# A hybrid encoder trunk on one core: a third unit of seven block products in each feed-forward layer, and the units spread over the second to sixth chunk

## The chip, the core and the metric

The kernel runs on one core of a Trainium2 chip. The metric is the device time of one execution in microseconds (us): 2188.74 is the median of three runs of the kernel before (2188.52 to 2188.94). The engines are TensorE (PE, matmuls; PEld is its loading of stationary operands), VectorE (DVE), ScalarE (ACT), GpSimd (POOL) and SyncE (SP, which issues the transfers of weights here). Each engine executes its own program in order, and engines wait for each other by semaphores.

## What is computed

Two layers on 256 tokens of width 2048: the first mixes by pooling and grouped-query attention, the second by a bidirectional mLSTM. Each is followed by a gated feed-forward part (FFN) with a depthwise convolution over three neighbouring tokens. All data is float32. The change touches the up-projection of the FFN alone:

```python
def conv_ffn(x, w_up, conv_w, conv_b, w_down):      # D_MODEL 2048, D_FF 5632
    u = x @ w_up                                    # (256, 2048) @ (2048, 2*5632)
    up = jnp.pad(u, ((0, 0), (1, 1), (0, 0)))
    u = c[0] * up[:, :-2] + c[1] * up[:, 1:-1] + c[2] * up[:, 2:] + conv_b
    gate, val = jnp.split(u, 2, axis=-1)
    return (jax.nn.silu(gate) * val) @ w_down       # (256, 5632) @ (5632, 2048)

for layer in range(2):
    ...
    x = x + mixed
    x = x + conv_ffn(rms_norm(x, norm_ffn[layer]), w_up[layer], ...)
```

## The kernel before

**Products in two parts.** Every float32 operand is split into a high part, which a matmul takes exactly, and the low rest. A product is three matmuls: high by high, high by low and low by high. For weights this is `Stream` (L65): it issues a chunk of 128 x 1024 weights (512 KB) on SP's queue into a tile `w` (L89), ACT copies the high part into `hl` (L112), and DVE subtracts to get the low part (L113). In the FFN seven chunks are loaded ahead and three split ahead of the one that PE uses (L1103); the chunks come in the order in which PE needs them.

**The FFN.** The 5632 inner columns are 44 *row tiles* of 128; a row tile is a gate part and a value part. They are cut into six K chunks of 4, 8, 8, 8, 8 and 8 row tiles (`FCH`, L33; numbered 0 to 5), since they are what the down-projection sums over. `up` (L928) computes one row tile for all 256 tokens with the weights stationary: 16 blocks of the width 2048, each with two matmuls of 512 columns and two of 256, 64 in all, four weight chunks. ACT and DVE then gather the sums (L391, L392), multiply by the tokens' norm (L936), and `tail` (L912) does the convolution, the gate and the split of the result (L917 to L926) into a gate tile `g`. `down` (L1074) multiplies a chunk's gate tiles with the down weights, in four blocks of 512 output columns, and adds into `x` (L401). Gate tiles of even and odd chunks use two buffers in turn (B0, B1).

**Units of seven products.** For four of a chunk's row tiles another way is there, `quads` (L978). It takes the tokens in two halves and the blocks of the width in pairs, so that the product is one of 2 x 2 blocks, and computes it with seven block products instead of eight, from sums of blocks. The sums of activations `sx` are made once for each layer by DVE and ACT (`sums`, L939, with L945 to L961), the sums of weights by DVE in the loaded chunk (`sums` of `Stream`, L93: a chunk of kind "sum" takes one addition of 512 columns, L99; one of kind "chain" two, L102 and L103). A unit has eight pairs of blocks in 28 *steps* of one weight chunk each: 16 of four products (p1, p5 and p6, p4 in turn, a chunk each), and 12 of the three others. A step is six matmuls of 512 columns. A unit's 28 chunks stand in place of the 16 of four row tiles. Its result comes out with the tokens on the partitions, in four accumulators that DVE and ACT combine (L1006 to L1027); `finish` (L1032) turns it by 16 transposes on PE, copies (L1041) and calls the same `tail`. A unit begins only when the tails of the one before are done (`late`, L991).

**The order.** PE's program is in the order in which the code is written (`manual_schedule`, L206). For the FFN `_ffn_plan` (L1192) writes it as a list: a *slot* is a quarter of a row tile (16 matmuls) or two blocks of a down-projection (12 matmuls), and after each slot stand the unit steps that fall to it. `UNITS` (L1189) has a unit for the last four row tiles of chunks 2 and 4, each with the chunk and the offset in slots where its steps begin and end; the steps are spread evenly between. The sequence of weight chunks follows the same plan (`_ffn_order`, L1239). Work of other engines that belongs to PE's progress is fed in by `Weave` (L135), a list of small tasks that come due while PE's program is written. The order of DVE's and ACT's instructions is set by the framework's scheduler from these programs; only the sums of weights and activations are pinned to the order of the code.

Of the kernel before, what the change touches and what calls it, by code (L numbers as in the profile page):

```python
# [10 lines left out]
F32R = mybir.dt.float32r  # L11
# [5 lines left out]
P = 128  # L17
D = 2048
S = 256
# [161 lines left out]
def trunk(ctx: ExitStack, tc: tile.TileContext, gx, xT, xn, call, catt, cml, weights, out):  # L181
    nc = tc.nc
    v, a, g, pe = nc.vector, nc.scalar, nc.gpsimd, nc.tensor
# [713 lines left out]
    def ffn_layer(layer, norm, nxt):  # L897
        with ExitStack() as es:
# [76 lines left out]
            def sum_of(j, p):  # L975
                return [sx[:, j, p, i, :] for i in range(2)]

            def quads(fs, gt, i0, name):  # L978

                def bank(j):  # L980
                    return psp.tile([P, 512], F32, tag="ps", name=f"p{j}_{name}")
# [29 lines left out]
                for p in range(m):  # L1011
                    hl = st.next()
                    product(b5, sum_of(3, p), hl, 0, False, p == m - 1)
                    product(b6, sum_of(2, p), hl, 512, False, p == m - 1)
                    if p == m - 1:
                        v.scalar_tensor_tensor(c21, b6, r1, c21, ALU.mult, ALU.add)
                        v.tensor_add(c22, c22, c21)
                        v.scalar_tensor_tensor(c21, b4, r1, c21, ALU.mult, ALU.subtract)
                        v.scalar_tensor_tensor(c12, b5, n0, c12, ALU.mult, ALU.add)
                    yield  # L1020
                    if p % 2:
                        hl = st.next()
                        for n in range(2):
                            product(b1, block_of(2 * (p - 1 + n) + 1, 0), hl, n * 512, False, p - 1 + n == m - 1)
                        if p == m - 1:
                            c11 = part(11)
                            a.activation(c11, b1, AF.Copy, scale=r0)  # L1027
                            wv.add(finish(c12, c22, fs[2:], gt, i0 + 2, name), 3.0)
                            wv.add(finish(c11, c21, fs[:2], gt, i0, name), 5.0)
                        yield  # L1030

            def finish(top, bottom, fs, gt, i0, name):  # L1032

                for n, f in enumerate(fs):
                    tr = psp.tile([P, 2, S], F32, tag="ps", name=f"tr{layer}_{f}")
                    for j in range(2):
                        for t, src in enumerate((top, bottom)):
                            c = (2 * j + n) * P
                            pe.transpose(tr[:, j, t * P : t * P + P], src[:, c : c + P], ident)
                    u = tp.tile([P, 2, S], F32, tag="tb", name=f"tb_{layer}_{f}")  # L1040
                    a.copy(u, tr)  # L1041
                    tail(u, f, gt, i0 + n)
                    yield 2.5
                late.discard((i0 - 4) % 4)
# [57 lines left out]
            wv.add(sums_ready(), 14.0)  # L1102
            st.la, st.sa, st.more = 7, 3, (lp(f"fw{layer}", 1), lp(f"fh{layer}", 1), st.at + len(_ffn_plan()))  # L1103
            gts, run, late = {}, {}, set()
            for step in _ffn_plan():
                kind, c = step[:2]
                if kind != "d" and c not in gts:
                    gts[c] = actp.tile([P, 8, 2, S], F32R, tag=f"B{c % 2}", name=f"g{layer}_{c}")
                key = step[:3]
                if key not in run:  # L1110
                    f0 = sum(FCH[:c])
                    run[key] = (up(f0 + step[2], gts[c], step[2]) if kind == "n" else
                                down(c, gts[c], step[2]) if kind == "d" else
                                quads([f0 + 4 + j for j in range(4)], gts[c], 4, f"{layer}_{c}"))
                next(run[key], None)
            for e in run.values():
                assert next(e, None) is None
# [68 lines left out]
    return np.concatenate(out)  # L1186


UNITS = {2: (1, 2, 3, -7), 4: (3, 2, 5, -7)}  # L1189


def _ffn_plan():  # L1192
# [168 lines left out]
```

## Time and profile before

| What | Value |
|---|---|
| Median of the runs | 2188.74 us |
| The profiled execution | 2188.64 us |
| Its span, from first to last instruction | 2186.3 us |
| Packets of SP's queue (the weights), share of 16 transfer engines' time | 61.4% |
| Traffic, mean over the span | 202 GB/s |
| Time to landing of a unit's 512 KB chunk, median | 4.0 us |
| Matmuls of the units (all kinds), now four units | 672 |
| First FFN layer's up-projection begins | at 255.94 us |

The profile is one execution on the chip. A busy time is the sum over an engine's instructions with overlaps counted once; matmul records overlap, since matmuls are pipelined, so lengths of PE's work are read from the chain of waits or from start to start. "idle before, releaser" is the time that an engine stood still just before a group, and what ended it. Names such as `hl` or `p` are tiles of the program with their numbers left out: `up` is the accumulator of a row tile, `dn` of a down-projection, `p` of a unit, `tr` of its transposes, `hl` a split weight chunk. L227 is the line of a helper that writes every matmul.

### The profile page before, as it was taken

The page shows a single profiled execution, that of the slowest core. Times are in us where ns is not written, and L with a number is a line of the kernel's source. Part 1 is how long each engine was busy: PE and PEld are TensorE (multiplying, and loading weights), DVE is VectorE, ACT ScalarE, POOL GpSimd, SP SyncE. Part 2 cuts the span into 40 slices and gives each one's busy share as a digit, 9 for nine tenths or more (in the row PEclk, how much of TensorE's full clock was granted, in tenths as well). Part 3 has the DMA queues.
Part 4 walks back from the last instruction along what each step waited for, and adds up shares of the span by engine and source line. Part 5 has one row for each costly group of instructions (what it writes and reads, how often), then busy time and mean ns, then how long its engine had stood idle before and what let it go on. Part 6 is the DMA issues. An engine that isn't in the chain of part 4 may idle for free.

```text
span 2186.3 us, 30347 instructions
## 1 busy us (share of the span) xinstructions
PE 2180.1 (100%) x11328; PEld 1861.1 (85%) x11328; DVE 1673.3 (77%) x2378; ACT 1229.4 (56%) x1744; POOL 29.2 (1%) x40
## 2 busy tenths in 40 slices
PE   9999999999999999999999999999999999999999
PEld 7888888888888888889888888888888888888887
DVE  7686798878887786666767676679987888778664
ACT  7665565656555565556555554556565655556552
POOL 0020000000000000000000000000000000000000
PEclk9999999999999999999999999999999999999999
DMA  9555557675676755557565555655677667676563
GB/s 323 181 168 174 183 186 231 229 230 195 229 226 221 226 195 192 186 161 205 160 202 179 181 179 176 196 183 181 233 231 226 198 220 233 221 222 196 193 189 125
DMA packets 124950, 440.88 MB, mean 202 GB/s; under 512 B 13850, under 2 KB 16194, under 8 KB 124802
## 3 DMA queue, kind: packets, MB, share of 16 engines
q1 hardware_dynamic: 121568, 434.93, 61.4%
q10 hardware_dynamic: 3074, 3.75, 0.8%
q8 instruction: 89, 1.46, 0.3%
q14 instruction: 59, 0.48, 0.1%
q0 software_dynamic: 160, 0.26, 0.0%
HBM read 436.74 MB, written 2.14 MB: 201 GB/s over the span
## 4 chain that ended last, share of the span: by engine, by line
PE 97%; DVE 2%; issue 0%; ACT 0%
PE up L227 34%; PE dn L227 21%; PE op L227 8%; PE p L227 7%; PE mv L227 4%; PE mq L227 4%; PE mk L227 4%; PE mo L227 4%; PE qproj L227 3%; PE pool L227 1%; PE kproj L227 1%; PE vproj L227 1%; DVE hl L113 1%; PE av L227 1%; PE qk L227 1%; PE end L227 0%
## 5 line engine op out<-in xcount | busy, mean ns | idle before, releaser
L113 DVE TENSOR_TENSOR hl<-w,hl 128x1024 fp32r<-128x1024 f32 (+1 forms) x820 | 992.6, 1218 | 357.6 <-ACT hl L112 350.8
L112 ACT CAST hl<-w 128x1024 fp32r<-128x1024 f32 (+1 forms) x819 | 852.4, 1048 | 662.1 <-PE up L227 137.3
L227 PE MATMUL up<-xx,hl 128*128 128x512 f32 (+1 forms) x4608 | 823.1, 337 | 0.0
L227 PEld LDWEIGHTS up<-xx,hl 128*128 128x128 f32 x4608 | 716.1, 188 | 109.1
L227 PE MATMUL dn<-hl,g 128*128 128x512 f32 x2064 | 480.9, 390 | 0.0
L227 PEld LDWEIGHTS dn<-hl,g 128*128 128x128 f32 x2064 | 385.0, 188 | 78.5
L227 PE MATMUL p<-hl,sx 128*128 128x512 f32 x384 | 103.5, 391 | 1.1 <-DVE hl L113 1.1
L391 ACT COPY tb_up<-up 128x512 f32<-128x512 f32 x72 | 42.2, 587 | 99.4 <-PE up L227 94.8
L917 ACT ACTIVATE y<-tb_up,cst 128x256 f32<-128x256 f32 x144 | 78.8, 595 | 32.6 <-DVE tb_up L936 30.4
L227 PE MATMUL mk<-xx,hl 128*128 128x512 f32 (+1 forms) x512 | 92.2, 338 | 0.0
L227 PE MATMUL mq<-xx,hl 128*128 128x512 f32 (+1 forms) x512 | 92.2, 337 | 0.0
L227 PE MATMUL mv<-hl,xx 128*128 128x512 f32 (+2 forms) x480 | 91.7, 350 | 0.0
L227 PE MATMUL op<-hl,cat 128*128 128x512 f32 x384 | 91.6, 393 | 0.0
L227 PE MATMUL mo<-hl,xx 128*128 128x512 f32 x384 | 90.5, 391 | 0.0
L227 PE MATMUL op<-hl,mcat 128*128 128x512 f32 x384 | 89.5, 392 | 0.0
L227 PEld LDWEIGHTS mq<-xx,hl 128*128 128x128 f32 x512 | 79.3, 188 | 11.6
L227 PEld LDWEIGHTS mk<-xx,hl 128*128 128x128 f32 x512 | 79.1, 188 | 11.4
L227 PEld LDWEIGHTS mv<-hl,xx 128*128 128x128 f32 x480 | 78.3, 189 | 11.2
L392 DVE TENSOR_TENSOR tb_up<-up,tb_up 128x512 f32<-128x512 f32 x72 | 49.8, 692 | 47.7 <-ACT tb_up L391 47.6
L227 PEld LDWEIGHTS op<-hl,mcat 128*128 128x128 f32 x384 | 71.5, 188 | 14.6
L227 PEld LDWEIGHTS mo<-hl,xx 128*128 128x128 f32 x384 | 71.0, 188 | 14.3
L227 PEld LDWEIGHTS op<-hl,cat 128*128 128x128 f32 x384 | 70.9, 188 | 14.1
(240 smaller groups left out, 1740.2 us busy)
## 6 DMA issues: line engine op xcount, KB each, us to landing
w<-in_up SPq DMA_DIRECT2D x288, 512.0 KB, 4.2
w<-in_dn SPq DMA_DIRECT2D x176, 512.0 KB, 4.2
w<-in_m_in SPq DMA_DIRECT2D x124, 512.0 KB, 4.1
w<-in_q SPq DMA_DIRECT2D x112, 512.0 KB, 4.0
w<-in_a_in SPq DMA_DIRECT2D x46, 512.0 KB, 4.4
w<-in_a_out SPq DMA_DIRECT2D x32, 512.0 KB, 3.4
w<-in_m_out SPq DMA_DIRECT2D x32, 512.0 KB, 3.4
w<-in_m_g SPq DMA_DIRECT2D x5, 432.0 KB, 3.5
```

The source lines that it names most:

```text
L112: (self.nc.vector.tensor_copy if i + c == 0 else self.nc.scalar.copy)(hl[:, 0, c : c + n], w[:, c : c + n])
L113: self.nc.vector.tensor_sub(hl[:, 1, c : c + n], w[:, c : c + n], hl[:, 0, c : c + n].bitcast(F32))
L227: pe.matmul(out_, lhsT, rhs, start=start, stop=stop, skip_group_check=True)
L391: a.copy(tb, ps[:, :, 1, :])
L392: v.tensor_add(tb, ps[:, :, 0, :], tb)
L917: a.activation(y[:, j, :], u[:, j, :], AF.Identity, scale=cw(tl, 1), bias=cw(tl, 3))
```

## The change

The change puts a third unit into each layer, for the last four row tiles of chunk 5, and gives all three new places: the first from two slots into chunk 1 to slot 20 of chunk 2, the second from slot 23 of chunk 2 to slot 2 of chunk 4, the third from slot 5 of chunk 4 to slot 24 of chunk 5. The last two slots in each entry of `UNITS` count from the start of the chunk named; before, -7 was seven slots ahead of it. A layer has then 84 steps and 216 slots where it had 56 and 232. The gate tile of a chunk is no longer taken at the first step that belongs to the chunk, but where it is first written (`g_of`).

```diff
-            def quads(fs, gt, i0, name):
+            def quads(fs, c, i0, name):
...
                             a.activation(c11, b1, AF.Copy, scale=r0)
+                            gt = g_of(c)
                             wv.add(finish(c12, c22, fs[2:], gt, i0 + 2, name), 3.0)
                             wv.add(finish(c11, c21, fs[:2], gt, i0, name), 5.0)
...
             gts, run, late = {}, {}, set()
+            def g_of(c):
+                if c not in gts:
+                    gts[c] = actp.tile([P, 8, 2, S], F32R, tag=f"B{c % 2}", name=f"g{layer}_{c}")
+                return gts[c]
+
             for step in _ffn_plan():
                 kind, c = step[:2]
-                if kind != "d" and c not in gts:
-                    gts[c] = actp.tile([P, 8, 2, S], F32R, tag=f"B{c % 2}", name=f"g{layer}_{c}")
                 key = step[:3]
                 if key not in run:
                     f0 = sum(FCH[:c])
-                    run[key] = (up(f0 + step[2], gts[c], step[2]) if kind == "n" else
+                    run[key] = (up(f0 + step[2], g_of(c), step[2]) if kind == "n" else
                                 down(c, gts[c], step[2]) if kind == "d" else
-                                quads([f0 + 4 + j for j in range(4)], gts[c], 4, f"{layer}_{c}"))
+                                quads([f0 + 4 + j for j in range(4)], c, 4, f"{layer}_{c}"))
                 next(run[key], None)
...
-UNITS = {2: (1, 2, 3, -7), 4: (3, 2, 5, -7)}
+UNITS = {2: (1, 2, 2, 20), 4: (2, 23, 4, 2), 5: (4, 5, 5, 24)}
```

What this does to the order is seen at three places. The first two are DVE's program where the first unit of the first layer begins, from the low half of chunk hl100 on. Names carry the chunk's number: hl101 is the split of w101, and so on; v0 and sx0 are the sums of activations. Before:

```order
L113 TENSOR_TENSOR hl100_2904<-w100_2795,hl100_2904 128x1024
L961 TENSOR_TENSOR sx0_2407<-v0_2595,sx0_2407 128x4x128 x2
L926 TENSOR_TENSOR g0_0_2415<-y0_2_2760,g0_0_2415 128x256
L956 TENSOR_TENSOR v0_2595<-v0_2595 128x512
L961 TENSOR_TENSOR sx0_2407<-v0_2595,sx0_2407 128x4x128
L936 TENSOR_TENSOR tb_up0_3_2862<-tb_up0_3_2862,R1_2530 128x512
L113 TENSOR_TENSOR hl101_2928<-w101_2818,hl101_2928 128x1024
L102 TENSOR_TENSOR w102_2840<-w102_2840,w99_2772 128x512
L961 TENSOR_TENSOR sx0_2407<-v0_2595,sx0_2407 128x4x128
L918 SCALAR_TENSOR_TENSOR y0_3_2866<-tb_up0_3_2862,cst_84,y0_3_2866 128x255 x2
L103 TENSOR_TENSOR w102_2840<-w102_2840 128x512
L113 TENSOR_TENSOR hl104_3006<-w104_2902,hl104_3006 128x1024
```

Here the unit's second chunk is w102, two quarter tiles after the first, w99. The same place after the change:

```order
L113 TENSOR_TENSOR hl100_2904<-w100_2795,hl100_2904 128x1024
L102 TENSOR_TENSOR w101_2818<-w101_2818,w99_2772 128x512
L961 TENSOR_TENSOR sx0_2407<-v0_2595,sx0_2407 128x4x128 x2
L926 TENSOR_TENSOR g0_0_2415<-y0_2_2760,g0_0_2415 128x256
L956 TENSOR_TENSOR v0_2595<-v0_2595 128x512
L961 TENSOR_TENSOR sx0_2407<-v0_2595,sx0_2407 128x4x128
L936 TENSOR_TENSOR tb_up0_3_2862<-tb_up0_3_2862,R1_2530 128x512
L103 TENSOR_TENSOR w101_2818<-w101_2818 128x512
L961 TENSOR_TENSOR sx0_2407<-v0_2595,sx0_2407 128x4x128
L918 SCALAR_TENSOR_TENSOR y0_3_2866<-tb_up0_3_2862,cst_84,y0_3_2866 128x255 x2
L920 SCALAR_TENSOR_TENSOR y0_3_2866<-tb_up0_3_2862,cst_84,y0_3_2866 128x255 x2
L113 TENSOR_TENSOR hl101_2930<-w101_2818,hl101_2930 128x1024
```

The second chunk is now w101, after one quarter tile; its two sums stand ahead of the last of sx, and its low half behind two L918 and two L920. In the second layer the rows are the same up to L103; then the low half of the chunk after the unit's second one (hl564) comes first, behind it the last sx and two L918, then that of the unit's second chunk (hl563), and the L920 behind that. DVE's program of the first layer goes on, after the change, with:

```order
L113 TENSOR_TENSOR hl102_2951<-w102_2840,hl102_2951 128x1024
L113 TENSOR_TENSOR hl103_2966<-w103_2879,hl103_2966 128x1024
L99 TENSOR_TENSOR w104_2902<-w104_2902 128x512
L392 TENSOR_TENSOR tb_up0_4_2988<-up0_4_2878,tb_up0_4_2988 128x512
L113 TENSOR_TENSOR hl105_3019<-w105_2928,hl105_3019 128x1024
L924 TENSOR_TENSOR y0_3_2866<-y0_3_2866 128x256
L113 TENSOR_TENSOR hl106_3042<-w106_2949,hl106_3042 128x1024
L102 TENSOR_TENSOR w107_2964<-w107_2964,w104_2902 128x512
L936 TENSOR_TENSOR tb_up0_4_2988<-tb_up0_4_2988,R1_2530 128x512
L113 TENSOR_TENSOR hl104_3005<-w104_2902,hl104_3005 128x1024
```

The unit's third chunk is w104, and its low half stands behind those of hl105 and hl106, which PE uses later. Before, the third was w105, and the row was hl102, hl103, hl105.

The third place is PE's program in chunk 5 of the first layer, at the second block of chunk 4's down-projection (`dn_4_1`). Before, the four blocks of it stood together:

```order
L227 MATMUL up_39_7523<-xx_126,hl_7526 128x256 x2
L227 MATMUL dn_4_1_7623<-hl_7547,g_4_5020 128x512 x12
L227 MATMUL dn_4_1_7623<-hl_7568,g_4_5020 128x512 x12
L227 MATMUL dn_4_1_7623<-hl_7589,g_4_5020 128x512 x12
L227 MATMUL dn_4_1_7623<-hl_7626,g_4_5020 128x512 x12
L227 MATMUL up_40_7694<-xx_126,hl_7643 128x512 x2
```

After the change steps of the third unit stand between them, and fewer row tiles around them:

```order
L227 MATMUL up_37_7570<-xx_126,hl_7606 128x256 x2
L227 MATMUL dn_4_1_7694<-hl_7627,g_4_6381 128x512 x12
L227 MATMUL p_0_5_6610<-hl_7648,xx_126 128x512 x6
L227 MATMUL dn_4_1_7694<-hl_7659,g_4_6381 128x512 x12
L227 MATMUL p_0_5_6611<-hl_7697,sx_2407 128x512 x3
L227 MATMUL p_0_5_6641<-hl_7697,sx_2407 128x512 x3
L227 MATMUL dn_4_1_7694<-hl_7714,g_4_6381 128x512 x12
L227 MATMUL dn_4_1_7694<-hl_7725,g_4_6381 128x512 x12
```

Each of the steps is a chunk more for SP, ACT and DVE in front of the next slot.

## The prediction

> **What bounds the kernel now.** I read the clock first, then the page's busy shares and its chain of waits, then the groups, then the timelines of TensorE (PE) and VectorE (DVE) around the units of seven products.
>
> ```profile
> core 0: 2186.3 us, clock 1.000
> PE 2180.1 (100%) x11328; PEld 1861.1 (85%) x11328; DVE 1673.3 (77%) x2378; ACT 1229.4 (56%) x1744; POOL 29.2 (1%) x40
> PE 97%; DVE 2%; issue 0%; ACT 0%
> L227 PE MATMUL p<-hl,sx 128*128 128x512 f32 x384 | 103.5, 391 | 1.1 <-DVE hl L113 1.1
> L113 DVE TENSOR_TENSOR hl<-w,hl 128x1024 fp32r<-128x1024 f32 (+1 forms) x820 | 992.6, 1218 | 357.6 <-ACT hl L112 350.8
> ```
>
> The granted clock is full, PE is busy all of the span, and 97% of the chain that ended last is PE. Both feed-forward (FFN) layers are a stream of matmuls with hardly a hole, so the time is PE's work plus what PE waits for. Among the units' products PE idles 1.1 us in all, and what ends the idling is DVE, making the low half of a weight chunk (L113). DVE is the runner-up: its 77% is an average, and in the first unit's stretch it is more:
>
> ```profile
> 310.20:515.10 204.90, 204.37 (x1055) 174.05 (x1053) 175.07 (x231) 119.20 (x151) 0.00 (x0) 1.00 0.71 227
> ```
>
> The columns are the stretch, its length, then busy time of PE, its weight loads, DVE, ACT and POOL, then clock, DMA share and GB/s. DVE is busy 175.1 of 204.9 us there (85%), ACT 58%. So every edit has two prices: PE time, which is the span, and DVE time, which becomes the span where DVE falls behind by more than the chunks split in advance.
>
> **What a unit saves on PE.** The chain of waits lists pieces (start, length, what) so that lengths add up without the overlap of matmul records:
>
> ```profile
> 340.21 5.56 PE up L227 x32
> 345.77 1.37 PE p L227 x6
> 347.14 5.56 PE up L227 x32
> 352.70 1.37 PE p L227 x6
> ```
>
> Half a row tile of the plain up-projection (32 matmuls) takes 5.56 us, so a tile 11.12 and the four tiles that a unit replaces 44.48. One step of a unit (a chunk, six matmuls) takes 1.365 (these two pieces read 1.37, others 1.36); 28 steps take 38.22. A unit also needs 16 transposes, which the plain tiles do not. PE's timeline where the first unit's are threaded into a tile:
>
> ```profile
> 517.82 0.85 PE L227 MATMUL up<-xx,hl 128*128 128x512 f32 x4
> 518.50 0.60 PE L1039 MATMUL tr<-cst,c 128*128 128x128 f32 x4
> 518.86 2.35 PE L227 MATMUL up<-xx,hl 128*128 128x512 f32 x12
> ...
> 524.75 0.60 PE L1039 MATMUL tr<-cst,c 128*128 128x128 f32 x4
> 525.11 5.13 PE L227 MATMUL up<-xx,hl 128*128 128x512 f32 x28
> ```
>
> Four groups of four transposes stand behind 4, 12, 4 and 12 up matmuls (the rows left out are the middle ones). From 517.82 to 525.11 are 7.29 us; the 32 up matmuls are half a tile, 5.56, so the 16 transposes cost 1.73. One unit in place of four tiles therefore saves 44.48 - 38.22 - 1.73 = 4.53 us of PE, and one per layer in two layers 9.06. This is the first term and the certain one: the products are the same instructions, and the last chunk's down-projections are untouched.
>
> The Trainium skill (TensorE: Matmul & The Clock Gate, Back-to-back issue gap) gives 512/2.4 + 2.5 = 216 ns and 109 ns for 256 columns. The trace's steps are longer (1.365 us over six is 0.2275). By the page a tile would be an estimated 10.40 us, a step 1.30, the saving 41.6 - 36.3 - 1.73 = 3.6 per unit, and the sum below 1.9 us less gained; rows decide.
>
> **What else a unit adds.** Twelve more chunks per unit pass SP's queue, ACT's cast, and DVE's subtraction, and 32 sums of 512 columns run on DVE. Removed with four tiles are four gathers (L391, L392) and four multiplications (L936). Whether that is hidden is DVE's question. The densest new stretch is the third unit: 28 steps over 51 quarter-tile slots, where the first unit now has 28 over 63. DVE's prices, from start to start, are in this timeline (start, length, then the instruction):
>
> ```profile
> 305.46 1.22 DVE L113 TENSOR_TENSOR hl<-w,hl 128x1024 fp32r<-128x1024 f32 x1
> 306.60 1.29 DVE L961 TENSOR_TENSOR sx<-v,sx 128x512 fp32r<-128x512 f32 x2
> 307.80 0.42 DVE L926 TENSOR_TENSOR g<-y,g 128x256 fp32r<-128x256 f32 x1
> 308.14 0.69 DVE L956 TENSOR_TENSOR v<-v 128x512 f32<-128x512 f32 x1
> ...
> 309.94 1.22 DVE L113 TENSOR_TENSOR hl<-w,hl 128x1024 fp32r<-128x1024 f32 x1
> 311.08 0.69 DVE L102 TENSOR_TENSOR w<-w,w 128x512 f32<-128x512 f32 x1
> 311.68 0.69 DVE L961 TENSOR_TENSOR sx<-v,sx 128x512 fp32r<-128x512 f32 x1
> 312.28 0.88 DVE L918 SCALAR_TENSOR_TENSOR y<-tb_up,cst,y 128x255 f32<-128x255 f32 x2
> ...
> 316.80 3.49 DVE L113 TENSOR_TENSOR hl<-w,hl 128x1024 fp32r<-128x1024 f32 x3
> ```
>
> So a subtraction takes 1.14 (309.94 to 311.08), an addition of 512 columns 0.60, two L918 0.79, an L926 or L924 0.34. The unit's own work is 28 x 1.14 + 32 x 0.60 = 51.1 us. The other 175.1 - 51.1 = 124.0 us of the first unit's stretch belong to 63 slots; 51 slots carry 100.4, so DVE has 151.5 us to do in the third unit's stretch. PE's time for it: (204.9 - 38.2) x 51/63 + 38.2 = 173.1. DVE would be at 88% there, ACT at 59% by the same scaling. The 79 chunks of 0.524 MB ask 239 GB/s, against 227 in the row above, and the page's slices show more than that without a wait for a transfer:
>
> ```profile
> GB/s 323 181 168 174 183 186 231 229 230 195 229 226 221 226 195 192 186 161 205 160 202 179 181 179 176 196 183 181 233 231 226 198 220 233 221 222 196 193 189 125
> ```
>
> So on average the added work lies beside PE: I cost it at nothing, but for two kinds of place, where DVE's work comes in a lump.
>
> **The starts of the first unit.** Here DVE also makes the sums of the activations (sx), and here PE waits today, once in each layer, at the unit's second step:
>
> ```profile
> 310.22 0.85 PE L227 MATMUL p<-hl,xx 128*128 128x512 f32 x3
> 310.91 0.84 PE L227 MATMUL p<-hl,sx 128*128 128x512 f32 x3
> 311.59 5.72 PE L227 MATMUL up<-xx,hl 128*128 128x512 f32 x32
> 317.15 0.40 PE L227 MATMUL p<-hl,sx 128*128 128x512 f32 x1
> 318.08 0.74 PE L227 MATMUL p<-hl,sx 128*128 128x512 f32 x2 [0.53 <-DVE hl L113]
> ```
>
> Matmuls of a product start 0.23 apart (0.69 for three); here 0.93 lie between the first and the second, so 0.70 are lost: the second matmul needs the low half, which DVE's L113 of 316.80 delivers at 318.02. The change brings the second step one quarter tile (2.78) nearer, and the order of DVE changes with it. I lay the new order (shown with the change) on today's prices, from the last instruction that both share (hl100, 305.46). Ahead of hl101 now stand L102 0.60, two sx 1.20, L926 0.34, L956, sx, L936, L103 and sx 0.60 each, 0.79 for two L918 and as much for two L920: it starts at 306.60 + 6.72 = 313.32 and ends at 314.54. PE's second step is due at 311.59 + 2.78 = 314.37, its second matmul at 314.60: no wait. PE leaves it at 315.74 and needs hl104 after two quarter tiles, at 321.30, the low half at 321.53. DVE starts hl104 last of a row: hl101, hl102, hl103, hl105, hl106 at 1.14, four of 0.60 (L99, L392, L102, L936) and L924, thus 313.32 + 5.70 + 2.40 + 0.34 = 321.76, and ends at 322.98. PE waits 1.45 there in place of 0.70.
>
> ```profile
> 1509.07 1.22 DVE L113 TENSOR_TENSOR hl<-w,hl 128x1024 fp32r<-128x1024 f32 x1
> ...
> 1513.82 0.85 PE L227 MATMUL p<-hl,xx 128*128 128x512 f32 x3
> ...
> 1520.75 0.40 PE L227 MATMUL p<-hl,sx 128*128 128x512 f32 x1
> 1521.68 0.72 PE L227 MATMUL p<-hl,sx 128*128 128x512 f32 x2 [0.53 <-DVE hl L113]
> ```
>
> The second layer (rows of DVE and PE together) loses 0.70 today too. There the second step's hl563 now stands behind hl564: hl562 is done with DVE's front at 1509.07 + 1.14 = 1510.21, hl563 starts 5.93 + 1.14 = 7.07 later and ends at 1518.50; the second matmul is due at 1513.82 + 1.37 + 2.78 + 0.23 = 1518.20, a wait of 0.3. What comes after I bound by nothing and by the first layer's 1.45, and take 0.7: a wait of about 1.0 in all. Together 2.45 where 1.40 are lost now: **+1.05**. The bounds are -1.40 (no wait at all) and +4.2 (each start waits a whole quarter tile, 2.78, against 1.40 for both).
>
> **The joints of the units.** By the plan a unit now begins five slots, 13.8 us, after the one before has ended; today it is twelve, 33 us. At a joint DVE has the ended unit's work to do: four tails (two L918, two L920, L924, L926: 2.26 each) 9.0, some four combinations (about 0.67 each, a little over an addition's price) 2.7, five subtractions 5.7, and up to 3.5 for a plain tile (L392 and L936 at 0.60, and a tail): 17.4 to 20.9. It falls 3.6 to 7.1 behind. Split ahead are three chunks, 8.3 us of PE at 2.78. So I take no wait, but the margin may be 1 us; the bound is one quarter tile, 2.78, at each of four joints. If that cover is gone, PE waits for L113 at the first steps of a unit, and behind them everything, since PE is in order.
>
> The other edit costs nothing: a chunk's gate tile is now taken by its first plain tile or by a unit's tails, not at the unit's first step. Half of the third unit runs while chunk 3's gates, in the same buffer, are still read by PE; it is the fifth chunk's plain tiles that take the buffer, as today, after the last of these reads. Nothing on PE waits for it.
>
> **The sum.** The profiled execution took 2188.64 us (span 2186.3), 0.10 under the median of the runs shown. 2188.64 - 9.06 + 1.05 + 0.10 = 2180.7; with 0.2 for the thin margin at the joints **2180.9**.
>
> **Rivals.** *(a) The joints wait a little*, about half a quarter tile (1.4) each: 2180.7 + 5.6 = 2186.3. For it speaks the thin margin; against it that no joint waits today and DVE has 12% of slack around them. *(b) VectorE becomes the bound:* it falls more than three chunks behind at each joint, and PE waits a whole quarter tile there: 4 x 2.78 = 11.1, with the starts at their bound 3.1 more, 2180.7 + 14.2 = 2194.9, slower than before. It decides from the point where the lump at a joint exceeds PE's 13.8 us by more than 8.3. For it speaks that the only waits of the whole stream are for L113; against it the 88%. *(c) VectorE's operations do not overlap:* each takes its whole recorded length, 0.08 more than I counted. hl104 then comes some 20 operations later by 1.6, and a joint's 25 operations add 2.0, some 1 us over the margin: 2180.7 + 2 x 1.6 + 4 x 1.0 = 2187.9, no change. The rows speak against it: 3.49 for three L113 of 1.22 each, 1.29 for two of 0.69.
>
> The Trainium skill (VectorE: DVE Perf Modes, The DRAIN you can't avoid) says that after every VectorE operation the pipeline drains before the next one starts, which, taken as whole lengths one behind the other, would be (c); by the rows the record of one operation runs on into the next.
>
> *(d) The starts no longer wait:* 2188.74 - 9.06 - 1.40 = 2178.3. It needs hl104 1.45 us earlier than the order puts it.
>
> **Chances.** The forecast 0.80 (its own range 2179.5 to 2183.0), (a) 0.09, (b) 0.06, (c) 0.02, (d) 0.03. A difference of 0.2% (4.4 us) is about what a measurement of this kernel can tell from no change: below 2184.4 is faster. Faster: forecast and (d), 0.83; same: (a) and (c), 0.11; slower: (b), 0.06. The range from 2179.0 to 2185.4 holds the forecast and the lighter half of (a).
>
> **What would show it.** PE's busy time falls by about 9 us; in the chain up falls by 8 tiles (89 us) and p rises by 56 steps (76 us), each at its old length. If steps or halves of tiles are longer than 1.365 and 5.56, the first term is wrong. Between PE's p matmuls there is one idle of 1.4 us, some 11 us after the first unit begins in the first layer, ended by L113, and smaller ones in the second. Idle of PE at the second and third units' first steps would be (a), and a row of such waits with DVE above 95% there (b). If PE waits for a transfer or for ACT, I have missed the mechanism. The prediction is wrong if the profile shows more than 4 us of PE idle in the two FFN layers.

## The result and the profile after

The changed kernel takes **2180.64 us** (median of six runs, 2180.56 to 2180.92); the kernel before took 2188.68 in six runs beside it. The ratio is 0.9963 with a 95% interval of 0.9951 to 0.9976: faster by 0.37%. Predicted were 2180.9. In the profiled executions the span went from 2186.3 to 2178.3 us, by 8.0.

The page of the changed kernel, its busy shares and its chain of waits:

```profile
span 2178.3 us, 30227 instructions
PE 2171.3 (100%) x11184; PEld 1850.7 (85%) x11184; DVE 1730.3 (79%) x2460; ACT 1252.7 (58%) x1776; POOL 29.2 (1%) x40
PE 97%; DVE 3%; issue 0%; ACT 0%; DVEq 0%
PE up L227 30%; PE dn L227 22%; PE p L227 10%; PE op L227 8%; PE mv L227 4%; PE mq L227 4%; PE mk L227 4%; PE mo L227 4%; PE qproj L227 3%; DVE hl L113 1%; PE pool L227 1%; PE kproj L227 1%; PE vproj L227 1%; PE av L227 1%; PE qk L227 1%; PE end L227 1%
```

PE's busy time fell by 8.8 (2180.1 to 2171.3), in the chain `up` fell from 34% to 30% of the span and `p` rose from 7% to 10%. DVE has 57 us more to do, and stands at 79% on average. The chain's pieces (start, length, what) in the first layer have the old lengths:

```profile
343.75 1.37 PE p L227 x6
345.12 5.56 PE up L227 x32
```

If the 9.06 us of PE work went as the sum said, PE must wait 9.06 - 8.0 = 1.06 us more than before. PE's timeline at the start of the first layer's first unit (start, length, instruction, and in brackets the idle time before it with what ended it):

```profile
314.32 0.98 PE L227 MATMUL p<-hl,sx 128*128 128x512 f32 x3
315.14 0.85 PE L227 MATMUL p<-hl,xx 128*128 128x512 f32 x3
...
321.40 0.40 PE L227 MATMUL p<-hl,xx 128*128 128x512 f32 x1
322.99 0.74 PE L227 MATMUL p<-hl,xx 128*128 128x512 f32 x2 [1.19 <-DVE hl L113]
```

At the third step 1.59 lie between two matmuls that otherwise start 0.23 apart: 1.36 are lost. At the second step (314.32) three matmuls take 0.82 instead of 0.69, another 0.13: there the loading of the second matmul's weights (PEld) waited 0.17 us for the low half. The bracket says 1.19 because the record of the first matmul, 0.40, runs on past the 0.23 at which the next could start; the start-to-start loss of such a gap is the bracket and 0.17. DVE's timeline shows the two low halves on which PE stood:

```profile
313.29 3.50 DVE L113 TENSOR_TENSOR hl<-w,hl 128x1024 fp32r<-128x1024 f32 x3
...
321.70 1.23 DVE L113 TENSOR_TENSOR hl<-w,hl 128x1024 fp32r<-128x1024 f32 x1
```

hl101 starts at 313.29 and hl104 at 321.70, where the prediction had laid them at 313.32 and 321.76. The second layer's first unit, PE again:

```profile
1514.15 0.40 PE L227 MATMUL p<-hl,sx 128*128 128x512 f32 x1
1514.73 0.73 PE L227 MATMUL p<-hl,sx 128*128 128x512 f32 x2 [0.19 <-DVE hl L113]
...
1528.49 0.40 PE L227 MATMUL p<-hl,sx 128*128 128x512 f32 x1
1529.33 0.73 PE L227 MATMUL p<-hl,sx 128*128 128x512 f32 x2 [0.44 <-DVE hl L113]
```

0.58 - 0.23 = 0.35 is lost at the second step and 0.84 - 0.23 = 0.61 at the fourth: 0.96, and with the first layer's 1.49 it is 2.45 us in all, 1.05 more than the 1.40 before, which agrees with the 1.06 left over above. Nothing else in the two FFN layers waits. The windows of the three units of the first layer (the stretch, its length, busy time of PE, weight loads, DVE, ACT and POOL, then clock, DMA share and GB/s):

```profile
310.20:505.00 194.80, 193.61 (x1003) 164.97 (x1002) 167.13 (x221) 112.81 (x143) 0.00 (x0) 1.00 0.69 229
520.00:716.00 196.00, 196.00 (x1003) 166.96 (x1002) 166.43 (x220) 113.50 (x145) 0.00 (x0) 1.00 0.68 228
733.00:906.00 173.00, 173.00 (x854) 146.28 (x853) 145.90 (x187) 98.91 (x122) 0.31 (x1) 1.00 0.70 231
```

The third unit's stretch is as long as worked out (173.0 for 173.1), DVE is at 145.9 of it (84%, 151.5 had been forecast), and PE is busy throughout.

### The profile page after: what moved, and what is told of

The parts are those of the page before. It is cut to its first block, busy times and chain, and to the rows that moved or that the text cites. A ratio compares the mean times of both kernels' runs of the same rounds, so it can differ in the third digit from the quotient of the medians.

```text
span 2178.3 us, 30227 instructions
## 1 busy us (share of the span) xinstructions
PE 2171.3 (100%) x11184; PEld 1850.7 (85%) x11184; DVE 1730.3 (79%) x2460; ACT 1252.7 (58%) x1776; POOL 29.2 (1%) x40
## 4 chain that ended last, share of the span: by engine, by line
PE 97%; DVE 3%; issue 0%; ACT 0%; DVEq 0%
PE up L227 30%; PE dn L227 22%; PE p L227 10%; PE op L227 8%; PE mv L227 4%; PE mq L227 4%; PE mk L227 4%; PE mo L227 4%; PE qproj L227 3%; DVE hl L113 1%; PE pool L227 1%; PE kproj L227 1%; PE vproj L227 1%; PE av L227 1%; PE qk L227 1%; PE end L227 1%
## 5 line engine op out<-in xcount | busy, mean ns | idle before, releaser
L113 DVE TENSOR_TENSOR hl<-w,hl 128x1024 fp32r<-128x1024 f32 (+1 forms) x844 | 1018.2, 1218 | 315.7 <-ACT hl L112 306.9
L112 ACT CAST hl<-w 128x1024 fp32r<-128x1024 f32 (+1 forms) x843 | 874.9, 1048 | 654.8 <-DVE w L99 105.3
L227 PE MATMUL up<-xx,hl 128*128 128x512 f32 (+1 forms) x4096 | 737.4, 337 | 0.0
L227 PEld LDWEIGHTS up<-xx,hl 128*128 128x128 f32 x4096 | 642.3, 188 | 99.2
L227 PE MATMUL dn<-hl,g 128*128 128x512 f32 x2064 | 487.0, 390 | 0.0
L227 PE MATMUL p<-hl,sx 128*128 128x512 f32 x576 | 155.3, 391 | 0.6 <-DVE hl L113 0.6
L227 PEld LDWEIGHTS p<-hl,sx 128*128 128x128 f32 x576 | 103.9, 188 | 20.0 <-DVE hl L113 1.4
L227 PE MATMUL p<-hl,xx 128*128 128x512 f32 x432 | 118.2, 391 | 1.2 <-DVE hl L113 1.2
L227 PEld LDWEIGHTS p<-hl,xx 128*128 128x128 f32 x432 | 77.8, 188 | 15.3 <-DVE hl L113 1.5
L917 ACT ACTIVATE y<-tb_up,cst 128x256 f32<-128x256 f32 x128 | 70.1, 595 | 27.5 <-DVE tb_up L936 23.6
```

The costliest lines, as they stand in the source:

```text
L112: (self.nc.vector.tensor_copy if i + c == 0 else self.nc.scalar.copy)(hl[:, 0, c : c + n], w[:, c : c + n])
L113: self.nc.vector.tensor_sub(hl[:, 1, c : c + n], w[:, c : c + n], hl[:, 0, c : c + n].bitcast(F32))
L227: pe.matmul(out_, lhsT, rhs, start=start, stop=stop, skip_group_check=True)
L917: a.activation(y[:, j, :], u[:, j, :], AF.Identity, scale=cw(tl, 1), bias=cw(tl, 3))
```

## The experiments

The theory (A): every unit more is worth 4.53 us of PE, and beside it only the waits at the first units' starts count; these come from DVE's lump there (sums of activations, sums of weights and low halves together), not from its average. Rivals: the gain comes from the new spacing rather than from the third unit; the waits have another cause; DVE's average is the limit. All runs go beside the kernel before, whose medians are 2188.6 to 2188.7. The tuples of `UNITS` give for each chunk the first slot's chunk and place and the last slot's, as in the diff.

### The two halves of the change, each alone

**e1**, the new places for two units, no third one:

```diff
-UNITS = {2: (1, 2, 2, 20), 4: (2, 23, 4, 2), 5: (4, 5, 5, 24)}
+UNITS = {2: (1, 2, 2, 20), 4: (2, 23, 4, 2)}
```

> The first two units of each layer at their new places, without the third; chunk 5 again has eight plain row tiles. Theory (the gain is the third unit's 4.53 us of PE per layer; the new places cost only the longer waits at the first unit's start, 2.46 us where 1.40 were): PE's work is that of the kernel before, so 2188.7 + 1.1 = 2189.8, with idle of PE only at the first unit's third step (about 1.4) and the like in the second layer. Rival 1 (closer units by themselves save time, the third unit is beside the point): below 2187. Rival 2 (the joint of the units, 5 slots, makes PE wait half a quarter tile or more): 2191.2 and up.

Measured: 2190.3 us (2190.23 to 2190.67), ratio 1.0008 [0.9999, 1.0017]. PE waits at the two starts alone, 1.16 and 1.19 us by the brackets, both ended by L113. So the new places alone do not gain; against the changed kernel, with the third unit as the only difference, e1 is 9.7 us slower. The sum's price is 9.06, and e1's gaps are 0.24 longer (1.16 + 1.19 + 2 x 0.17 = 2.69 against 2.45); the remaining 0.4 is within the interval. The rival of the spacing falls.

**e2**, the third unit in the old table:

```diff
-UNITS = {2: (1, 2, 2, 20), 4: (2, 23, 4, 2), 5: (4, 5, 5, 24)}
+UNITS = {2: (1, 2, 3, -7), 4: (3, 2, 5, -7), 5: (5, -4, 5, 24)}
```

> The third unit added, the first two left at their places of the kernel before; the third must then follow the second's end and run through 28 slots of chunk 5, about one step per slot. Rival (PE's sum decides alone, VectorE does not matter): 2188.7 - 9.06 = 2179.6, even better than the change. Theory (VectorE decides once its work nears PE's): in the 28 slots PE has 38.2 + 166.7 x 28/63 = 112.3 us, VectorE 51.1 + 124.0 x 28/63 = 106.2, that is 95%, on top of the lump of the joint before it (3.6 to 7.1 behind) and with only three chunks of cushion; it cannot make good what it loses, so PE waits for L113 at several steps of the third unit, 4 to 10 us per layer: 2187 to 2199, the gain lost or worse. The first unit's wait is 0.70 in each layer again.

Measured: 2201.75 us (2201.65 to 2202.82), ratio 1.0061 [1.0047, 1.0075]: slower than before, and by more than expected. The third unit's 28 steps now crowd into 28 slots, and PE's idle time is no longer only DVE's doing. Two rows of PE there, with the windows behind them:

```profile
824.06 0.50 PE L227 MATMUL p<-hl,sx 128*128 128x512 f32 x1 [1.87 <-ACT hl L112]
826.31 0.73 PE L227 MATMUL p<-hl,sx 128*128 128x512 f32 x2 [1.74 <-DVE hl L113]
```

```profile
820.00:827.30 7.30, 3.69 (x18) 2.78 (x18) 6.21 (x8) 3.22 (x4) 0.00 (x0) 1.00 0.81 264
827.30:830.70 3.40, 3.40 (x11) 2.81 (x10) 1.83 (x2) 1.38 (x2) 0.00 (x0) 0.51 0.93 351
```

First the chunk's high half (ACT, L112) is late, then its low half. In all there are 15 gaps and 14.9 us. That is not the whole price: behind the two gaps the clock column reads 0.51 for 3.4 us, and 0.50 for 6.8 us at a second place. Half a clock for 10.2 us costs up to 5.1. Neither half of the change gains by itself; the third unit brings the PE time, and the new places are what makes room for it.

### What makes PE wait at the starts

**e3**, the first unit of each layer begins four slots later, behind the sums of activations:

```diff
-UNITS = {2: (1, 2, 2, 20), 4: (2, 23, 4, 2), 5: (4, 5, 5, 24)}
+UNITS = {2: (1, 6, 2, 20), 4: (2, 23, 4, 2), 5: (4, 5, 5, 24)}
```

> The change with the first unit's steps beginning six slots into chunk 1 instead of two; its end and the other units stay. Theory (the waits at the start come from VectorE's lump of activation sums, sx): four slots later (11 us) the lump is over, the waits of 1.49 and 0.97 vanish and nothing else changes, since VectorE is at 51.1 + 124.0 x 54/63 = 157.4 of 181.1 us (87%) in the first unit's stretch: 2180.6 - 2.5 = 2178.1. Rival (the waits come from the order in which VectorE takes the chunks, or from the unit's density, wherever the unit begins): they move along, 2180.6 or more.

Measured: **2177.84 us** (2177.72 to 2178.05), ratio 0.9951 [0.9938, 0.9963], better than both kernels. Its page:

```profile
PE 2170.4 (100%) x11184; PEld 1849.9 (85%) x11184; DVE 1730.3 (80%) x2460; ACT 1253.1 (58%) x1776; POOL 29.2 (1%) x40
PE 100%; DVE 0%; issue 0%
L227 PE MATMUL p<-hl,sx 128*128 128x512 f32 x576 | 154.5, 390 | 0.0
```

The same work on every engine, the chain all PE, no idle time before the units' products. DVE begins the last of its sums of activations at 312.22 here, and the unit's first step comes at 321.36.

**e6**, the changed kernel without the weights' sums on DVE, so that its units multiply plain blocks:

```diff
-            if kind == "sum":
-                pin(add(r, r, l))
-                self.sum = r
-            if kind == "chain":
-                pin(add(l, l, self.sum))
-                pin(add(r, r, l))
```

> The change without the sums of weight blocks on VectorE (L99, L102, L103 left out: the units multiply plain blocks), PE's and ScalarE's instructions as in the change: 32 x 0.60 = 19 us less VectorE work per unit. Theory (the waits at the first unit's start are VectorE's, late by its queue): hl104 comes 4 x 0.60 earlier in the first layer, more than the 1.36 that PE waits there, and in the second layer the two waits of 0.36 and 0.61 are less than the sums ahead of them: all idle goes, 2180.6 - 2.5 = 2178.1, the time of e3 by another way. Nothing more is gained with 57 us less VectorE work per layer, since PE's work is the rest. Rival (VectorE's load sets the time also elsewhere, hidden in longer PE steps): below 2175. Rival 2 (the start's place or order, not the work, makes the wait): 2180.6.

Measured: 2177.82 us (2177.69 to 2177.86), ratio 0.9951 [0.9936, 0.9965]; PE idles nowhere in the FFN layers, with the units where the change has them. Moving the start away from the lump and taking part of the lump away give the same time within 0.02 us. The waits come from the coincidence of the two, and the whole 2.8 us with them (2.45 by the gaps).

**e9**, e3 with the weights' sums on GpSimd (POOL):

```diff
-            pin, add = self.tc.keep_in_program_order, self.nc.vector.tensor_add
+            pin, add = self.tc.keep_in_program_order, self.nc.gpsimd.tensor_add
```

> e3 with the sums of weight blocks (L99, L102, L103) added by GpSimd in place of VectorE. An addition of 271 columns takes 0.64 us there in the kernel before, so about 1.2 us for 512 by columns. Theory (PE's work is all that is left in e3, which has no idle of PE): no change, 2177.8, if GpSimd's longer sums stay within the chunks loaded ahead. Rival (GpSimd's sums come too late, or slow VectorE down while both read): PE waits for L113 or ScalarE's L112 at unit steps, 2180 and up; L113 longer than 1.22.

Measured: 2177.73 us (2177.5 to 2178.15), ratio 0.995 [0.9934, 0.9967]: no change against e3. It is no test of less work on DVE, though: with the 192 sums on POOL DVE is busy for 1759.4 us, against 1730.3 in e3, which makes them itself, and 1624.0 in e6, where nobody makes them. Its other instructions take longer beside POOL's (the last section); only e6 shows that less work on DVE buys nothing where PE does not wait.

**e5**, the changed kernel with a second subtraction of 256 columns for 24 of the 28 chunks of each unit, those that get a sum:

```diff
+            if kind != 'plain':
+                self.nc.vector.tensor_sub(hl[:, 1, c : c + 256], w[:, c : c + 256], hl[:, 0, c : c + 256].bitcast(F32))
```

> The change, with a quarter of each unit chunk's low half (256 of 1024 columns) subtracted a second time into the same place: 28 more instructions of 0.34 us on VectorE per unit, nothing else. Rival (VectorE at 85% has slack, so 9.5 us more per unit, 90%, stay hidden): 2180.6, at most 1 us more at the starts. Theory (the averages do not matter; after each joint VectorE is within a fraction of a microsecond of PE): some eight unit chunks lie between a joint and the tightest place some 20 us behind it, 2.7 us more against a margin below 1 us, so about 2 us of new idle at each of four joints, and 1 more at each start: 2180.6 + 8 + 2 = 2190.6 (2186 to 2197), the change's gain gone.

Measured: 2200.69 us (2200.36 to 2203.03), ratio 1.0058 [1.0043, 1.0073]: 20 us more than the changed kernel, the direction expected and above the range. 144 instructions (the expectation counted 168) of 0.42 us, 60 us on DVE, make ten gaps of PE with 15.9 us, all ended by the new line (L115): 3.8 in four in the first layer's first unit, 3.99 at the second layer's start, and 8.1 in five, 12 to 25 us behind the beginning of a second or third unit. PE's timeline of the longest and the windows around it:

```profile
1521.30 0.40 PE L229 MATMUL p<-hl,sx 128*128 128x512 f32 x1
1525.68 1.22 PE L229 MATMUL p<-hl,sx 128*128 128x512 f32 x2 [3.99 <-DVE hl L115]
1526.70 1.48 PE L229 MATMUL p<-hl,xx 128*128 128x512 f32 x3
1527.98 6.00 PE L229 MATMUL up<-xx,hl 128*128 128x512 f32 x32
```

```profile
1520.00:1525.00 5.00, 1.69 (x10) 1.20 (x8) 5.00 (x9) 2.59 (x4) 0.00 (x0) 1.00 0.40 114
1525.00:1530.00 5.00, 4.32 (x15) 3.56 (x16) 5.00 (x10) 3.75 (x6) 0.00 (x0) 0.66 0.70 215
```

Three matmuls behind the gap take 1.28 from start to start instead of 0.69: the gap is paid again in a slow clock. That happens twice, 3.4 us each, so up to 3.4 are lost by it; with 15.9 of gaps and 10 x 0.17, on the 2177.8 without a wait, it makes 2198.8 of the 2200.7.

### The joints between units

**e4**, three slots between two units of a layer, where the change has five:

```diff
-UNITS = {2: (1, 2, 2, 20), 4: (2, 23, 4, 2), 5: (4, 5, 5, 24)}
+UNITS = {2: (1, 2, 2, 20), 4: (2, 21, 4, 2), 5: (4, 3, 5, 24)}
```

> The change with the second and third unit beginning two slots earlier, so that three slots instead of five lie between units; ends as they were. Theory (at a joint VectorE falls behind and lives on three split chunks, 8.3 us): its lump is 15.1 to 18.6 us against 8.3 of PE, so it falls 6.8 to 10.3 behind; PE waits 0 to 2 at each of four joints, about 1 on average: 2184.6 (2181 to 2189), all idle of PE at the first steps of the second and third unit, ended by L113. Rival (the cushion is far larger than the lump, five slots were no edge): 2180.6, no idle there.

Measured: 2185.56 us (2185.42 to 2185.8), ratio 0.9986 [0.9977, 0.9995]: 4.9 us more than the change, about the size expected, by another cause. PE and, behind it, ACT at the first joint:

```profile
515.23 0.95 PE L227 MATMUL p<-hl,xx 128*128 128x512 f32 x3
517.05 0.97 PE L227 MATMUL p<-hl,sx 128*128 128x512 f32 x3 [0.87 <-ACT tb L1042]
...
525.14 0.97 PE L227 MATMUL p<-hl,xx 128*128 128x512 f32 x3 [0.99 <-ACT tb L1042]
```

```profile
516.43 0.57 ACT L1042 COPY tb<-tr 128x512 f32<-128x512 f32 x1
...
524.51 0.58 ACT L1042 COPY tb<-tr 128x512 f32<-128x512 f32 x1
```

Both gaps end as a copy of ACT does (516.43 + 0.57 = 517.00; 524.51 + 0.58 = 525.09). The copy (L1042) takes the ended unit's transposes out of an accumulator bank; until then the new unit's next product has no bank to write to. No weight chunk was late there: each time a product of the same chunk had just run without waiting. The second layer's first joint shows the same pair; the second joint of each layer shows no gap at all.

**e7**, the same with the tails of the ended unit allowed earlier:

```diff
-                            wv.add(finish(c12, c22, fs[2:], gt, i0 + 2, name), 3.0)
-                            wv.add(finish(c11, c21, fs[:2], gt, i0, name), 5.0)
+                            wv.add(finish(c12, c22, fs[2:], gt, i0 + 2, name), 1.0)
+                            wv.add(finish(c11, c21, fs[:2], gt, i0, name), 3.0)
```

> e4 (joints of three slots) with the transposes of an ended unit written into PE's program two microseconds of its planned time earlier (the delays 3.0 and 5.0 of L1029 and L1030 made 1.0 and 3.0). In e4 PE's idle at the joints was ended by ScalarE's copy of the transposes: their accumulator banks are the ones that the next unit's p6 and p4 need. Theory A (the transposes come too late on PE, so the banks do): the copies come up to 2 us earlier and the four pairs of waits (0.87 + 0.99) go: about 2181.5. Theory B (the copies wait for their turn behind the tails of VectorE and ScalarE, so the banks come free when that lump is done, however early the transposes are): waits move but stay, 2184 to 2187.

Measured: 2186.54 us (2186.34 to 2188.07), ratio 0.9993 [0.9983, 1.0002]. The delay in the plan is not the cause. Three of the four groups of transposes come 1.4 to 2.8 us earlier than in e4 (the first at 506.57 instead of 509.39, the last at 514.82 as before), and gaps ended by the copy remain, 1.33 and 2.19 us, one in each layer; one of 1.3 for L113 comes up at another place. That the copies wait for room in the two buffers of the tails is argued from the order of ACT's rows and was not tried; at the longer gap the copy stands in ACT's program behind two casts that had themselves waited 2.58 us for PE. The run left one clean row, a single gap ahead of a slow clock:

```profile
1724.73 0.84 PE L227 MATMUL p<-hl,sx 128*128 128x512 f32 x3
1727.76 1.25 PE L227 MATMUL p<-hl,xx 128*128 128x512 f32 x3 [2.19 <-ACT tb L1042]
```

```profile
1728.30:1731.70 3.40, 3.40 (x11) 2.83 (x10) 2.98 (x6) 1.76 (x3) 0.00 (x0) 0.50 0.49 154
```

### How far it carries: a fourth unit

**e8**, four units per layer from the second to the sixth chunk:

```diff
-UNITS = {2: (1, 2, 2, 20), 4: (2, 23, 4, 2), 5: (4, 5, 5, 24)}
+UNITS = {2: (1, 6, 2, 1), 3: (2, 6, 3, 9), 4: (3, 14, 4, 16), 5: (4, 21, 5, 24)}
```

> A unit for the last four row tiles of chunk 3 too, four units per layer of 34 to 36 slots each with joints of five, the first beginning six slots into chunk 1 as in e3. Rival (PE's sum decides): 2177.8 - 9.06 = 2168.8. Theory (VectorE decides where a unit and the tails of the one before leave it no slack): per unit VectorE has 51.1 + 35 x 124.0/63 = 120.0 and the ended unit's tails 11.7, together 131.7 us, PE 38.2 + 35 x 166.7/63 + 1.7 = 132.5: 99%, with a lump at each joint that can no longer be made good. PE waits at the first steps of the second to fourth unit and at the starts, 3 to 6 us each, eight places: 2168.8 + 24 to 48, that is 2193 to 2217, slower than with three and than the kernel before.

Measured: 2231.21 us (2228.31 to 2233.25), ratio 1.019 [1.0173, 1.0207], over the expected range. The group of the units' products, by lines (busy, mean ns, idle and what ended it):

```profile
L227 PE MATMUL p<-hl,sx 128*128 128x512 f32 x768 | 214.0, 399 | 37.2 <-DVE hl L113 21.7 <-ACT hl L112 15.5
```

The first unit's first gap, in the timelines of DVE, of ACT and of PE:

```profile
331.76 0.69 DVE L99 TENSOR_TENSOR w<-w 128x512 f32<-128x512 f32 x1
...
338.95 1.22 DVE L113 TENSOR_TENSOR hl<-w,hl 128x1024 fp32r<-128x1024 f32 x1
```

```profile
332.53 2.94 ACT L112 CAST hl<-w 128x1024 fp32r<-128x1024 f32 x3 [2.22 <-issue]
```

```profile
335.52 0.51 PE L227 MATMUL p<-hl,sx 128*128 128x512 f32 x1 [1.81 <-ACT hl L112]
340.22 1.22 PE L227 MATMUL p<-hl,sx 128*128 128x512 f32 x2 [4.19 <-DVE hl L113]
```

And windows there, and of the first layer's FFN:

```profile
333.00:338.60 5.60, 1.22 (x5) 0.44 (x3) 5.60 (x10) 2.89 (x4) 0.00 (x0) 1.00 0.48 182
338.60:345.40 6.80, 5.18 (x14) 4.31 (x15) 5.59 (x8) 2.50 (x3) 0.00 (x0) 0.50 0.76 255
...
335.00:910.00 575.00, 559.91 (x2754) 472.29 (x2755) 497.94 (x660) 333.76 (x429) 0.00 (x0) 0.98 0.70 230
```

ACT's lateness is DVE's too: its casts begin when DVE's sum is done (331.76 + 0.69 = 332.45), then the low half follows on DVE (338.95 + 1.22 = 340.17), and PE goes on at 340.22. DVE is busy in all of the 5.60 us of the first window. There are 23 such gaps with 38.5 us, all in the first 16 of a unit's 28 steps, for which DVE makes 24 of the unit's 32 sums, and nine stretches at half clock with 47.8 us. PE is busy in 40.3 of these, which loses about 20. With 0.17 for each gap that is 2168.6 + 38.5 + 3.9 + 20.1 = 2231.1, near the 2231.21 (2233.21 in the profiled execution); 2168.6 is the time of e11, which does not wait.

**e11**, the same without the weights' sums (L99, L102, L103):

> e8 with the weight sums left out (the units multiply plain blocks), so neither VectorE nor GpSimd makes them. Theory (VectorE's total decided in e8): as in the run with the sums on GpSimd or a little better, 2169 to 2178. Rival (banks and tails at the joints decide): 2200 and up. The difference to the run with GpSimd is what GpSimd's sums cost in lateness or in VectorE's speed.

Measured: 2168.57 us (2168.36 to 2168.81), ratio 0.9908 [0.9893, 0.9923]. The window of the first layer's FFN:

```profile
335.00:890.00 555.00, 555.00 (x2785) 470.80 (x2784) 433.90 (x543) 342.37 (x432) 0.00 (x0) 1.00 0.75 240
```

PE is busy in all of the 555 us, at 240 GB/s. Two units more than e3 and 9.27 us less: the price of a unit holds again. Joints, accumulator banks and transfers allow four units; what e8 lacks lies in the sums, in the first steps of a unit. A sum costs DVE's time, and it stands between a chunk's landing and its cast; e11 takes away both, so how much each of the two counts is not shown. On the average DVE had the time: e8's 497.9 us of DVE are 90% of the 555 that PE would need.

**e10**, four units with the sums on GpSimd (the edits of e8 and e9):

> e8 (four units per layer) with the weight sums on GpSimd. Theory (e8 was slow for VectorE's 99%): VectorE's work per unit falls by 19.2 to 112.5 us against PE's 132.5, 85% as in the change, so most of e8's waits go and with them the halved clock behind them: PE's sum 2168.8 plus 0 to 12 at the joints: 2169 to 2181, faster than e3 if the joints are kind. Rival 1 (the joints' accumulator banks and tails, not VectorE's total, made e8 slow): 2200 and up still. Rival 2 (GpSimd cannot keep up): its 128 sums of 1.2 us are 154 us per layer, 28% of the 565 us, so only their lateness could matter: waits for L112, 2185 to 2200.

Measured: 2200.28 us (2197.32 to 2205.14), ratio 1.0055 [1.004, 1.007]; the forecast failed. The time is that of the first rival (the joints), but e11 has the same joints and does not wait. PE has 16 gaps with 18.5 us, and three stretches of 3.4 us at half clock. Groups of e10, POOL's most frequent addition and, from the page, the busy times and DVE's low halves:

```profile
L99 POOL TENSOR_TENSOR w<-w 128x512 f32<-128x512 f32 x128 | 230.1, 1798 | 549.3 <-DMA w<-in_q 314.1 <-DVE hl L113 147.0 <-DVE y L918 28.7
```

```profile
PE 2173.1 (99%) x11040; PEld 1841.8 (84%) x11040; DVE 1811.7 (82%) x2286; ACT 1276.5 (58%) x1808; POOL 544.6 (25%) x296
L113 DVE TENSOR_TENSOR hl<-w,hl 128x1024 fp32r<-128x1024 f32 (+1 forms) x868 | 1147.4, 1337 | 264.7 <-ACT hl L112 259.8
```

An addition takes 1.80 to 2.29 us on POOL, by its line, and the low half beside it 1.337 instead of 1.218. DVE hands over 256 sums (177 us at 0.69), and yet it is busy for 1811.7 us, more than in e8 (1789.1), which makes them on DVE, and 167 more than in e11 (1644.7), which makes none: nearly all of it comes back as slower work, 103 us of it in the low halves (868 x 0.119). So four units gain only where the sums cost nothing, and no version of four that computes all of the reference beat e3.

## Why the prediction was right

- **The saving on PE, 9.06.** Held three times: as 8.0 of span with gaps of PE that are 1.05 us longer in all, as 9.7 between e1 and the change, and as 9.27 between e3 and e11. The pieces kept their lengths.
- **The starts, +1.05.** Held in place, cause and size: 2.45 us where 2.45 had been forecast, 1.49 in the first layer (forecast 1.45) and 0.96 in the second (1.0). The order laid on today's start-to-start prices gave hl104's start within 0.06 us. The guess in it was the 0.7 after the second step in the second layer; it came as 0.61 at the fourth. That it came so near is luck, since nothing had been laid out behind the second step. e3 and e6 show the cause in two independent ways.
- **The joints, 0.2 and no wait.** No wait came, and the 0.2 was not paid: 2180.7 without it is nearer to the 2180.64. The margin was thin, as said. A tight place of the change lies some 20 us behind the joint at 520, in DVE's and PE's rows:

```profile
537.00 1.23 DVE L113 TENSOR_TENSOR hl<-w,hl 128x1024 fp32r<-128x1024 f32 x1 [0.75 <-ACT hl L112]
...
539.34 2.35 DVE L113 TENSOR_TENSOR hl<-w,hl 128x1024 fp32r<-128x1024 f32 x2
...
541.15 0.84 PE L227 MATMUL p<-hl,sx 128*128 128x512 f32 x3
```

The first of the two low halves ends at about 540.56, and the second matmul, which by the order of the rows takes it, starts at 541.38, 0.8 us later (at the like places behind other joints 0.5 to 0.8). But DVE had stood idle for 0.75 us before 537.00, waiting for a cast: it had made good the joint's lump by then, so the 0.8 us is not what the lump left over, and that it is near the 1 us of the forecast is luck. The joint itself lasts 15.6 us (504.91 to 520.49) and not 13.8, since the ended unit's transposes stand in it. The reasoning was incomplete in another way too: it named L113 as what gives way when a joint gets shorter, and in e4 it was the accumulator banks, held by transposes that ACT had not copied out. That bound lay beside the one that was worked out, and had not been looked for.
- **DVE's load, 88%.** Over-sized: 84%. The first unit's stretch, from which it was scaled, has more plain row tiles to a slot than the third's: its 11 multiplications (L936) and 24 L918 scale to 8.9 and 19.4 for 51 slots, and the third unit's stretch has 7 and 16. The 239 GB/s came as 231 for the same stretch. Neither changed the answer.
- **The rivals.** (a) and (b) fell for want of any idle time at the joints; (c) fell on the 3.50 for three low halves of 1.22 to 1.23; (d) fell with the 2.45 us of waiting, and its 2178.3 is nearly what e3 and e6 took without it, 2177.84 and 2177.82. The price of (b) was too low, though: it counted the idle time and not the clock, which e2, e5 and e8 paid on top. e8's own forecast had DVE nearly full, and 90% with bursts was enough.

## What to carry to other kernels

Where one engine is busy all of the span, price an edit by that engine's start-to-start times; here a gain of 7.8 us was forecast and 8.0 came. Then ask where the second-busiest engine gets its work in a lump while the first one needs it ahead of time: an average of 85 or 90% tells nothing of that, its program order laid on start-to-start prices does, and moving the start by four slots gave 2.8 us more here without any work less. List every resource that the closest pair of stages shares, the accumulator banks among them, before calling one of them the limit.

## What the hardware showed beyond that

**A wait of about 2 us can be paid twice.** After one gap of 2.19 us (e7), or two of 1.87 and 1.74 close together (e2), the granted clock was 0.50 for 3.4 us, elsewhere for 6.8 us (e2, e8), so that up to 1.7 or 3.4 us were lost besides the gap. The gaps of 0.87 and 0.99 us (e4), of 1.19 (the change) and one alone of 1.66 (e5) left it at 1.00. The Trainium skill (TensorE: Matmul & The Clock Gate, HAM oscillation) gives as its rule that PE should have no idle gap over about 3.4 us, and names a window of that length, at half clock after an idle one. The two levels and the length agree with these rows, the rule does not: 2.19 us sufficed.

The length of the gap does not decide alone. Two gaps of e10 are alike, 2.08 us, ended at 515.29, and 2.07, ended at 1725.15; behind the first the clock is halved, behind the second it is not:

```profile
512.33:515.75 3.42, 1.34 (x6) 0.80 (x6) 3.42 (x5) 1.35 (x2) 1.10 (x1) 1.00 0.35 132
515.75:519.16 3.41, 3.41 (x10) 2.63 (x9) 3.41 (x5) 2.02 (x3) 0.50 (x1) 0.50 0.75 232
...
1720.66:1724.07 3.41, 2.42 (x11) 1.69 (x9) 3.41 (x5) 0.01 (x1) 2.51 (x2) 1.00 0.63 223
1724.07:1727.49 3.42, 2.33 (x10) 1.95 (x11) 3.42 (x5) 1.83 (x4) 0.00 (x0) 1.00 0.39 135
```

The windows are not chosen freely: within an execution all stretches at half clock begin whole multiples of 3.413 us apart (in e8 at 338.65, 533.21, 662.92 and 843.82, which are 57, 95 and 148 of them behind the first). On this grid the first gap falls into one window, in which PE is busy for 1.34 us, and the second is spread over two, with 2.42 and 2.33. So it seems to be PE's work in a fixed window that sets the clock of the next one; that is argued from these rows, and no run moved a gap on purpose. The ten executions of e7 would fit: six took 2186.3 to 2186.6 us with a mean clock of 1.000, and four, the profiled one among them, 2187.8 to 2188.1 with 0.999.

**POOL beside DVE slows both.** In e9 the low halves took 1.303 us, in e10 1.337, without POOL's additions 1.218; POOL's additions, 1.28 us at the shortest, took 1.80 to 2.29 by their means. The Trainium skill (SBUF — State Buffer, Who interferes with whom) says that a VectorE instruction with two inputs in SBUF contends with a GpSimd one that reads SBUF; L113 has two, and the rows agree. The loss is not confined to L113: e10's DVE is busy for 167 us more than e11's, of which the low halves are 103. It is not spread evenly either: in e10 the low half at 332.24 takes 1.73 us beside an addition of POOL (330.71 to 332.88), and the one at 330.16 takes 1.21.
